# One store of early sums becomes sixteen, and moves from the end of the DMA queue to behind the fourth load

## The chip, the cores and the metric

The kernel runs on one core of a Trainium2 chip. The metric is the device time of one execution in microseconds; lower is better. The times are medians over runs, and a profile of one execution goes with them.

## The reference

`x` has the shape 32 x 512 x 1024 in float32, 67.1 MB. Each row of 1024 values is clamped at zero from below and summed:

```python
def reference(x):
    relu_x = np.maximum(x, 0)
    return np.sum(relu_x, axis=-1).astype(np.float32)
```

The output has 16384 sums, 65.5 KB. So nearly all of the traffic is the reading of `x` from HBM, and every byte of it is used once.

## The kernel before, in words

The rows are dealt out to the 128 partitions of SBUF. The first 2048 rows are the first block: partition p holds rows 16p to 16p+15. The other 14336 rows are dealt out likewise, 112 to a partition. The 128 columns of the tile `res` (128 partitions x 128 float32) hold the sums: columns 0 to 15 are those of the first block, 16 to 125 follow, and the last two columns come from the very end of the kernel.

The program is written by hand engine by engine; no scheduler moves anything. Each engine works through its own list in order, and semaphores tie the lists together.

- **Loads.** All of them are issued by SP (SyncE, line 103), in one hardware queue. Seven loads of 8.4 MB, 16 rows of 4 KB for each partition, go in turn into the three buffers `io0`, `io1` and `io2` (`NBUF` is 3). From the fourth on, a load waits until ScalarE and VectorE have read what its buffer held before; the list `freed` keeps the counts for that, and `freed[0]` is the pair of counts at which the first block's sums are complete. Here the wait is placed on VectorE's semaphore `dve`. Behind the seven follow six smaller ones: 8 rows, 4 rows, and four pieces of the last 4 rows.
- **Arithmetic of the large loads.** ScalarE clamps a buffer in place (`clamp`, line 144), in one instruction of 16 rows or in two of 8 or 7, and VectorE sums each of them over the row (`total`, line 152).
- **Arithmetic of the small loads.** Single rows are split between the engines: on ScalarE clamp and sum are one instruction (`act_row`, line 159), on VectorE too (`dve_row`, line 167). The last row is cut into pieces that ScalarE (line 121), VectorE (lines 126 and 254) and, for the clamp of one piece, GpSimd (line 234) share.
- **Stores.** SP issues three (line 115), all of them in the same hardware queue as the loads and behind the last of these: columns 0 to 15, columns 16 to 125, and the last two columns. In SP's list a wait for ScalarE's count stands ahead of each of the first two (line 114), and a wait for VectorE's count is part of the store itself.

So SP's list is: three loads; four loads, each of which waits for VectorE; the load of 8 rows, which waits as well; five small loads; store, store, store; and a last wait until the semaphore `stored` has counted 16 for every store.

A DMA of 128 partitions raises its semaphore in 16 steps, one for each DMA engine that has finished its part. The trace keeps a time for each of these steps; they are called landings here.

The call that issues the first block's sums, behind the six small loads, and the calls around it are:

```python
    store(0, ROWS, freed[0][0], sems.dve, freed[0][1])
    store(ROWS, NT - ROWS - 2, sums_act, sems.dve, sums_dve)
```

Of the kernel before, what the change touches and what calls it, by code (L numbers as in the profile page):

```python
# [7 lines left out]
P = 128  # L8

ROWS = 16  # L10
NBUF = 3
# [14 lines left out]
MIDDLE_ACT, END_ACT = 214, 321  # L26

EARLY = 1


def kernel(tc: tile.TileContext, x: bass.AP, out: bass.AP):
    nc = tc.nc
    sems = Semaphores(tc)

    tc.close()
    tc.compile()
    nc.cur_bb = nc.bb_map[tc.start_bb_name]
    body = nc.cur_bb.bb.instructions
    ends = list(body)
    body.clear()  # L40
    n_stores = relu_sum(nc, sems, x, out)
    body.extend(ends)


    nc.cur_bb = nc.bb_map[tc.start_bb_name + "_end"]
    nc.cur_bb.bb.instructions.clear()
    nums = sorted(s.num for s in (*sems.loads, sems.act, sems.dve))
    cleared = range(nums[0], nums[-1] + 1)
    assert len(cleared) == len(nums)
    nc.sync.sem_clear(cleared)  # L50
    nc.sync.wait_ge(sems.stored, 16 * n_stores).then_inc(sems.stored, -16 * n_stores)
    open_without_barrier(tc, EARLY)

# [11 lines left out]
def relu_sum(nc, sems: Semaphores, x: bass.AP, out: bass.AP):  # L65
# [23 lines left out]
    def rows(m, n):  # L89
        if m < ROWS:  # L90
            return xf[:, m : m + n, :]
        return xv[:, m - ROWS : m - ROWS + n, :]

    def sums(m, n):
        if m < ROWS:
            return of[:, m : m + n], res[:, m : m + n]
        return ov[:, m - ROWS : m - ROWS + n], res[:, m : m + n]
# [3 lines left out]
    def load(dst, src, after=None):  # L101
        nonlocal n_load
        dma = nc.sync.dma_start(out=dst, in_=src)  # L103
        if after:
            dma.wait_op(sems.dve, after[1], "sem-ge")
        dma.then_inc(sems.loads[n_load], 16)
        n_load += 1
        return sems.loads[n_load - 1]

    def store(m, n, act, sem, count):  # L110
        nonlocal n_store
        dst, src = sums(m, n)
        if act:
            nc.sync.wait_ge(sems.act, act)
        nc.sync.dma_start(out=dst, in_=src).wait_op(sem, count, "sem-ge").then_inc(
            sems.stored, 16
        )
        n_store += 1

    def act_part(ap, accum_out, after):  # L120
        nc.scalar.activation(out=ap, in_=ap, func=RELU, accum_out=accum_out).wait_op(  # L121
            *after, "sem-ge"
        ).then_inc(sems.end, 1)
# [15 lines left out]
    def clamp(ap, loaded):  # L139
        nonlocal n_act  # L140
        if n_act == 0:
            nc.scalar.preload_act_table(RELU).wait_op(loaded, 16, "sem-ge")  # L142
            loaded = None
        i = nc.scalar.activation(out=ap, in_=ap, func=RELU)  # L144
        if loaded is not None:
            i.wait_op(loaded, 16, "sem-ge")
        i.then_inc(sems.act, 1)
        n_act += 1

    def total(ap, m, n):  # L150
        nonlocal n_dve
        nc.vector.tensor_reduce(  # L152
            out=res[:, m : m + n], in_=ap, axis=mybir.AxisListType.X, op=ADD
        ).wait_op(sems.act, n_act, "sem-ge").then_inc(sems.dve, 1)
        n_dve += 1

    def act_row(ap, accum_out, loaded):
        nonlocal n_act
        i = nc.scalar.activation(out=ap, in_=ap, func=RELU, accum_out=accum_out)  # L159
        if loaded is not None:  # L160
            i.wait_op(loaded, 16, "sem-ge")
        i.then_inc(sems.act, 1)
        n_act += 1

    def dve_row(ap, accum_out, loaded):
        nonlocal n_dve
        i = nc.vector.tensor_scalar(  # L167
            out=ap,
            in0=ap,
            scalar1=0.0,  # L170
            scalar2=None,
            op0=MAX,
            op1=ADD,
            accum_out=accum_out,
        )
        if loaded is not None:
            i.wait_op(loaded, 16, "sem-ge")
        i.then_inc(sems.dve, 1)
        n_dve += 1

    freed = []
    m = 0
    for j in range(NB):
        buf = bufs[j % NBUF]
        loaded = load(buf[:, :, :], rows(m, ROWS), j >= NBUF and freed[j - NBUF])
        c = 0
        act_waits = dve_waits = loaded
        for n in TWO[j]:
            clamp(buf[:, c : c + n, :], act_waits)
            total(buf[:, c : c + n, :], m + c, n)  # L190
            act_waits = None
            c += n
        for _ in range(ACT[j]):
            act_row(buf[:, c, :], res[:, m + c : m + c + 1], act_waits)
            act_waits = None
            c += 1
        for _ in range(DVE[j]):
            dve_row(buf[:, c, :], res[:, m + c : m + c + 1], dve_waits)
            dve_waits = None
            c += 1  # L200
        assert c == ROWS
        freed.append((n_act, n_dve))
        m += ROWS
# [4 lines left out]
    for n in TAIL:  # L208
# [12 lines left out]
    src = rows(m, 4).rearrange("p c d -> p (c d)")  # L221
# [13 lines left out]
        out=clamped, in0=clamped, scalar1=0.0, scalar2=None, op0=MAX  # L235
    ).wait_op(loaded, 16, "sem-ge").then_inc(sems.end, 1)
    for lo, hi, n, first, second in (
        (end, 4 * D, END_ACT, 2 + n_last, 3 + n_last),
        (head, middle, MIDDLE_ACT, 0, 1),
    ):  # L240
        loaded = load(flat[:, at + lo : at + hi], src[:, lo:hi])
        act_part(flat[:, at + lo : at + lo + n], last[:, first : first + 1], (loaded, 16))
        dve_part(flat[:, at + lo + n : at + hi], last[:, second : second + 1], (loaded, 16))
# [2 lines left out]

    store(0, ROWS, freed[0][0], sems.dve, freed[0][1])
    store(ROWS, NT - ROWS - 2, sums_act, sems.dve, sums_dve)  # L250


# [2 lines left out]
        out=clamped,  # L255
# [5 lines left out]
        accum_out=res[:, NT - 2 : NT - 1],  # L261
    ).wait_op(*all_there, "sem-ge").then_inc(sems.end, 1)
    act_part(last[:, 2 + LAST_DVE :], res[:, NT - 1 : NT], all_there)
    store(NT - 2, 2, 0, sems.end, 16 + 5 + 2)
    return n_store


def open_without_barrier(tc: tile.TileContext, n_loads: int):

    SP = mybir.EngineType.SP
    blocks = tc.nc.main_func.blocks
    opening = blocks[0].instructions
    body = next(b for b in blocks if b.name == tc.start_bb_name).instructions
    for i in list(opening):
        if isinstance(i, (mybir.InstDrain, mybir.InstEventSemaphore)):
            opening.remove(i)
    loads = [i for i in body if i.engine == SP][:n_loads]
    for i in loads:  # L280
        assert isinstance(i, mybir.InstDMACopy)
        body.remove(i)
    at = next(n for n, i in enumerate(opening) if i.engine == SP)
    opening[at:at] = loads
# [30 lines left out]
```

## Time and profile before

| what | value |
|---|---|
| median of 3 runs | 160.91 us (160.89 to 160.95) |
| span of the profiled execution | 159.7 us |
| median of the runs less that span | 1.2 us |
| VectorE busy | 118.8 us, 74% of the span |
| ScalarE busy | 103.6 us, 65% |
| GpSimd busy | 1.0 us, 1% |
| DMA packets | 2304, 67.18 MB, mean 421 GB/s |
| read from and written to HBM | 67.11 MB and 0.07 MB |

The profile is of one execution. Its span runs from the first of the kernel's own instructions to the last; the time of a run has in it also what lies before and behind, so the median is read beside the span and not as the same thing. In the timeline, SP's rows stand for the issue of a DMA only; when its data has arrived is told by the landings. DMA issues have in the page a median time from issue to landing, and this includes the wait in the queue behind earlier DMAs: the store of the first block's sums took 31.0 us by that count, the last store, which meets empty queues, 1.4 us.

The page's row of DMA occupation in 40 slices goes over 16 engines; packet records in the trace have a start, a duration and a size each, without the number of the engine.

### The profile page before, as it was taken

What the parts mean: (1) busy time and instruction counts of PE and PEld (TensorE: products, weight loads), DVE (VectorE), ACT (ScalarE), POOL (GpSimd) and SP (SyncE); (2) the same over time, 40 slices, a digit from 0 to 9 for tenths busy, and PEclk for the clock granted to TensorE, in tenths of its full rate; (3) what the DMA queues carried; (4) which work ended last, traced back from release to release, by engine and by line L of the source; (5) the groups of instructions that cost most, each with busy time, mean ns of one, the idle gap of its engine ahead of it and who ended that gap; (6) DMA issues with size and microseconds to landing.
All of it is one profiled execution on the core that took longest, in us unless ns stands there. A gap on an engine that the chain in (4) does not pass through costs nothing.

```text
span 159.7 us, 125 instructions
## 1 busy us (share of the span) xinstructions
DVE 118.8 (74%) x44; ACT 103.6 (65%) x53; POOL 1.0 (1%) x5
## 2 busy tenths in 40 slices
DVE  0000000006999799999999999999999799999986
ACT  0000049993699808996099951999329993496995
POOL 0000000000000000000000000000000000000001
DMA  7996996996997997979969969969969969898993
GB/s 263 525 525 263 525 509 279 525 509 279 525 476 312 525 443 345 525 328 460 525 279 509 525 263 525 525 263 525 509 279 525 492 295 525 353 435 386 407 409 128
DMA packets 2304, 67.18 MB, mean 421 GB/s; under 512 B 640, under 2 KB 768, under 8 KB 1024
## 3 DMA queue, kind: packets, MB, share of 16 engines
q1 hardware_dynamic: 2304, 67.18, 98.0%
HBM read 67.11 MB, written 0.07 MB: 421 GB/s over the span
## 4 chain that ended last, share of the span: by engine, by line
DVE 45%; DMA 45%; ACT 9%; SPq 1%; issue 0%
DMA io<-in_x_dram 45%; DVE res L152 43%; ACT io L144 9%; DVE io L167 1%; SPq L103 1%; DVE io L126 1%; DVE io L254 0%
## 5 line engine op out<-in xcount | busy, mean ns | idle before, releaser
L152 DVE TENSOR_REDUCE res<-io 128x8 f32<-128x8192 f32 (+2 forms) x10 | 101.1, 10175 | 38.9 <-ACT io L144 38.9
L144 ACT ACTIVATE io<-io 128x8192 f32<-128x8192 f32 (+2 forms) x10 | 81.8, 8218 | 25.9 <-DMA io<-in_x_dram 25.9
L159 ACT ACTIVATE io<-io 128x1024 f32<-128x1024 f32 x18 | 18.8, 1043 | 6.6 <-DMA io<-in_x_dram 6.6
L167 DVE TENSOR_SCALAR_CACHE_REDUCE io<-io 128x1024 f32<-128x1024 f32 x14 | 16.2, 1214 | 0.5 <-DMA io<-in_x_dram 0.4
L142 ACT ACT_TABLE_LOAD x1 | 1.3, 1283 | 22.0 <-DMA io<-in_x_dram 22.0
L159 ACT ACTIVATION_READ_ACCUMULATOR io<-io 128x1 f32 x18 | 3.4, 187 | 0.0
L234 POOL TENSOR_SCALAR io<-io 128x254 f32<-128x254 f32 x1 | 0.8, 840 | 155.1 <-DMA io<-in_x_dram 155.1
L167 DVE DVE_READ_ACCUMULATOR io<-io 128x1 f32 x14 | 1.1, 82 | 0.0
L126 DVE TENSOR_SCALAR_CACHE_REDUCE io<-io 128x552 f32<-128x552 f32 (+1 forms) x2 | 1.1, 596 | 0.0
L121 ACT ACTIVATE io<-io 128x321 f32<-128x321 f32 (+1 forms) x2 | 0.9, 426 | 0.1
L254 DVE SCALAR_TENSOR_TENSOR io<-last,io 128x254 f32<-128x254 f32 x1 | 0.4, 425 | 0.0
L121 ACT ACTIVATION_READ_ACCUMULATOR io<-io 128x1 f32 x2 | 0.4, 187 | 0.0
L121 ACT ACTIVATE last<-last 128x153 f32<-128x153 f32 x1 | 0.3, 332 | 0.0
L121 ACT ACTIVATION_READ_ACCUMULATOR last<-last 128x1 f32 x1 | 0.2, 187 | 0.0
L126 DVE DVE_READ_ACCUMULATOR io<-io 128x1 f32 x2 | 0.2, 84 | 0.0
L299 POOL MEMSET const-bfloat16-1.0<- 128x1 bf16 x1 | 0.1, 101 | 0.0
L299 POOL MEMSET const-uint8-127<- 128x1 uint8 x1 | 0.1, 101 | 0.0
L299 POOL MEMSET const-float32-0.0<- 128x1 f32 x1 | 0.1, 99 | 0.2 <-issue 0.2
L299 POOL MEMSET const-float32-1.0<- 128x1 f32 x1 | 0.1, 98 | 0.0
L254 DVE DVE_READ_ACCUMULATOR io<-last,io 128x1 f32 x1 | 0.1, 83 | 0.0
## 6 DMA issues: line engine op xcount, KB each, us to landing
io<-in_x_dram SPq DMA_DIRECT2D x1, 4096.0 KB, 23.8
io<-in_x_dram SPq DMA_DIRECT2D x1, 2048.0 KB, 28.3
io<-in_x_dram SPq DMA_DIRECT2D x1, 1151.0 KB, 30.6
io<-in_x_dram SPq DMA_DIRECT2D x1, 436.5 KB, 31.2
io<-in_x_dram SPq DMA_DIRECT2D x1, 259.0 KB, 31.4
last<-in_x_dram SPq DMA_DIRECT2D x1, 201.5 KB, 31.4
io<-in_x_dram SPq DMA_DIRECT2D x7, 29.1
out_dram<-res SPq DMA_DIRECT2D x1, 55.0 KB, 1.6
```

The lines of the kernel that those rows point to most:

```text
L103: dma = nc.sync.dma_start(out=dst, in_=src)
L121: nc.scalar.activation(out=ap, in_=ap, func=RELU, accum_out=accum_out).wait_op(*after, "sem-ge").then_inc(sems.end, 1)
L126: i = nc.vector.tensor_scalar(out=ap, in0=ap, scalar1=0.0, scalar2=None, op0=MAX, op1=ADD, accum_out=accum_out,)
L142: nc.scalar.preload_act_table(RELU).wait_op(loaded, 16, "sem-ge")
L144: i = nc.scalar.activation(out=ap, in_=ap, func=RELU)
L152: nc.vector.tensor_reduce(out=res[:, m : m + n], in_=ap, axis=mybir.AxisListType.X, op=ADD).wait_op(sems.act, n_act, "sem-ge").then_inc(se ...
L159: i = nc.scalar.activation(out=ap, in_=ap, func=RELU, accum_out=accum_out)
L167: i = nc.vector.tensor_scalar(out=ap, in0=ap, scalar1=0.0, scalar2=None, op0=MAX, op1=ADD, accum_out=accum_out,)
L234: nc.gpsimd.tensor_scalar(out=clamped, in0=clamped, scalar1=0.0, scalar2=None, op0=MAX).wait_op(loaded, 16, "sem-ge").then_inc(sems.end, 1)
L254: nc.vector.scalar_tensor_tensor(out=clamped, in0=last[:, : 2 + LAST_DVE], scalar=0.0, in1=clamped, op0=MAX, op1=ADD, accum_out=res[:, NT ...
L299: nc = _bacc.Bacc("TRN2", target_bir_lowering=False, num_devices=1)
```

## The change

The store of the first block's sums (columns 0 to 15 of `res`, 64 bytes of each partition) no longer stands behind the last load. A new function issues it directly behind the fourth load, in 16 stores of consecutive partitions: 15 of them, then 14, 13 and so on down to 1, and then the last 8. Together these are the 128 partitions. The same bytes go to the same places. Each store has its own wait for VectorE's count and adds its 16 to `stored`; a wait for ScalarE's count stands once ahead of all of them. The lists of the other engines are unchanged, and so is the order of the loads among themselves.

```diff
+PARTS = [15, 14, 13, 12, 11, 10, 9, 8, 7, 6, 5, 4, 3, 2, 1, 8]
...
+    def store_by_parts(done):
+        nonlocal n_store
+        dst, src = sums(0, ROWS)
+        nc.sync.wait_ge(sems.act, done[0])
+        p = 0
+        for n in PARTS:
+            nc.sync.dma_start(out=dst[p : p + n], in_=src[p : p + n]).wait_op(
+                sems.dve, done[1], "sem-ge"
+            ).then_inc(sems.stored, 16)
+            n_store += 1
+            p += n
+        assert p == P
...
         loaded = load(buf[:, :, :], rows(m, ROWS), j >= NBUF and freed[j - NBUF])
+        if j == NBUF:
+            store_by_parts(freed[0])
...
-    store(0, ROWS, freed[0][0], sems.dve, freed[0][1])
     store(ROWS, NT - ROWS - 2, sums_act, sems.dve, sums_dve)
```

## The prediction

> **What bounds the kernel now.** I read the page first, then the chain of waits, the sync engine's own waits, its timeline, and last the trace's records of single DMA packets and landings. The page's queue row and two stretches of the windows view (columns: DVE, ACT, POOL busy with counts, clock, DMA share, GB/s):
>
> ```profile
> span 159.7 us, 125 instructions
> q1 hardware_dynamic: 2304, 67.18, 98.0%
> ```
>
> ```profile
> 100.00:137.00 37.00, 36.05 (x5) 27.65 (x8) 0.00 (x0) 1.00 0.98 425
> 137.00:155.00 18.00, 17.93 (x27) 15.63 (x30) 0.00 (x0) 1.00 1.00 426
> ```
>
> The 16 DMA engines are occupied for 98% of the span, and in the windows after 100 us nothing is left of them. VectorE is nearly as full there, but the page shows it at 74% over the span, and in the chain of waits the last stretch hangs on DMA again:
>
> ```profile
> 124.87 30.59 DMA io<-in_x_dram
> 155.46 0.02 issue
> 155.48 1.23 DVE io L167 x2
> 156.71 1.07 DVE io L126 x4
> 157.78 0.02 issue
> 157.80 0.43 DVE io L254 x2
> ```
>
> From 155.46 on each step starts as its load lands. The packet records say the same more sharply: every engine runs its 64 KB packets at 2.42 us each, the next one starting at the end of the one before, from 1.0 us to the last load. So the end is: the last landing of the last load (157.75), 0.5 us of arithmetic, the last store (issue 158.26, landing 159.66). A load's 16 landings, one an engine, are not level. Counted back from the latest engine, those of the last load are 0.58, 0.50, 0.48, 0.46, 0.45, 0.43, 0.42, 0.41, 0.41, 0.39, 0.39, 0.33, 0.30, 0.27, 0.21 and 0 us. One engine is always last, by 0.27 us at the first load and 0.21 at the last. It got its lag at the start (its first packet begins at 1.40 us and takes 3.30, where no other ends so late) and goes at the common pace afterwards. Delay on any other engine is free up to its figure in this list; delay on the latest one is paid in full.
>
> **The change, part by part.** *Removed from the tail: one store of 128 packets of 64 bytes.* In the tail it is issued at 126.91 and lies in every ring behind the last load. Its own landings (157.35 to 157.92) come 0.17 to 0.20 us after the last load's on the same engine, and nobody waits for them before 159.66. The final store, issued at 158.26, meets empty rings: the second store landed by 158.29, and the final one's packets begin at 159.09. So taking it away frees nothing on the path. Could it hold back the last load's landing? Between a load's last packet record and its landing lie 0.46 us on the latest engine for the last load, 0.42 to 0.50 for the six before it, 0.34 to 0.39 for the first load. I take 0; the bound for a gain is 0.46 - 0.34, 0.1 us.
>
> *Added on SP: 16 issues between the fourth and the fifth load.* The timeline of SP:
>
> ```profile
> 54.42 0.33 SPq L103 DMA_DIRECT2D io<-in_x_dram  x1
> ```
>
> ```profile
> 72.46 0.33 SPq L103 DMA_DIRECT2D io<-in_x_dram  x1
> ```
>
> ```profile
> 124.02 2.28 SPq L103 DMA_DIRECT2D io<-in_x_dram  x5
> 126.34 0.44 SPq L103 DMA_DIRECT2D last<-in_x_dram  x1
> 126.91 0.40 SPq L115 DMA_DIRECT2D out_dram<-res  x1
> ```
>
> The stores wait for the same counts of ScalarE and VectorE that have just released the fourth load, so none of the 17 waits (one for ScalarE, 16 for VectorE) waits. Issues back to back start 0.48 us apart (124.39 to 126.34, four of them). 16 x 0.48 = 7.7 us: SP is done at 54.8 + 7.7 = 62.5. What is queued behind is the fifth load, and VectorE releases its buffer only at 72.46. That is 10 us of cover. A second cover follows: engines have the fourth load to work on until 79.0 to 79.6, and a packet starts 1.0 us after its issue (first load), so the fifth load could go out 5.5 us later still. The stores may cost 23/16 = 1.45 us each on SP before an engine idles. I take 0. Later loads wait for VectorE as before, with growing reserve (the next is issued at 89.64 and reached at 98.3). The 16 x 17 more counts on the final semaphore come long before 159.66, and that wait is one instruction either way.
>
> *Added in the rings: the packets, now ahead of the fifth load.* This is where the change can reach the end, since whatever an engine does there shifts all its later packets. The only prices shown are those of the store in the tail: 64-byte packets start 7 ns apart on an engine and the closing 4-byte packet takes 6 to 7 ns more (their durations, 11 and 9 ns, overlap). Each of the 16 stores brings one closing packet to each engine that it uses. How a store of fewer than 128 partitions is spread no row shows; every DMA of before has 128 and lands on 16 engines. Bounds: one packet per engine, where the busiest engine gets 16 x (7 + 6) = 0.21 us and the idlest 0; evenly, 8 x 7 + 16 x 6 = 0.15 us on each; everything on one engine, 128 x 7 + 16 x 6 = 0.99 us. I take the first, since 128 partitions land as 8 to each of 16 engines, one landing an engine. With sizes from 15 down to 1 and then 8 the shares then run from 16 packets to none, mean 8. The latest engine could be any of them, so it pays 0 to 0.21 us, as a middle value 8 x 13 ns = 0.10 us. Even the worst other engine ends at most 0.21 - 0.21 = 0 behind it.
>
> [...] The trace shows one late engine but no number for it, and its packets are not slower after the first one.
>
> *Sum.* 0 (tail) + 0 (SP) + 0.10 (rings) on the profiled 159.7 us of span; the median of the runs, 160.91, lies 1.2 us above that span, outside of which nothing changes. 160.91 + 0.10 = 161.0. The two bounds of this case, 160.8 (a gain of 0.1) and 161.12 (0.21), both lie within 0.2% (0.32 us), about what a measurement of this kernel can tell from no change.
>
> **Rivals.**
>
> *Each store's completion holds its engine (slower).* In the tail, a store's landing follows the landing of the load ahead of it by 0.17 us or more, though the closing packets are recorded only 0.06 us apart. Read as a store that can't finish until what is ahead has, 16 stores in a row on one engine take 16 x 0.17 = 2.7 us instead of 0.21. Less the lead of that engine (0 to 0.58) this ends 2.1 to 2.7 us later: 163.0 to 163.6. It decides from 0.056 us a store (16 x 0.056 = 0.58 + 0.32) if the busiest engine is the earliest one, and from 0.32 / 16 = 0.02 us if it is the latest. For: the latency to HBM is real, and 16 closings in a row are not seen anywhere. Against: closings of loads hold nothing (a load of 8 packets takes 19.35 us a period, 8 x 2.417 = 19.34), and in the tail the second store's packets on the latest engine start at about 157.7, before the first store's landing there at 157.92. The other reading, that a write to HBM is answered 0.11 us later than one to SBUF while the engine goes on, fits as well. Chance 0.21.
>
> [...]
>
> *The fixed time of each store is served in sequence.* The last store takes 1.4 us from issue to landing; 16 of those on one engine, 22 us, would give about 183 us. [...] Against: the closings above. Chance 0.02.
>
> *A whole store goes to one engine.* 0.99 us, less a lead of 0 to 0.58: 161.3 to 161.9. For: odd sizes such as 13 and 11 have no precedent in the trace. Against: 128 rows are dealt out in equal shares. Chance 0.10.
>
> *SP is held back.* At 126.91 eight DMAs are unfinished and SP still issues in 0.4 us, so eight are accepted; the change puts up to 18 in the rings. If nine were too many, the seventh store would go out at 60.65 (a load lands), the other nine after 80.0, and 9 x 0.48 + 0.33 + 1.0 us put the fifth load's first packet at 85.7, where the engines ran dry at 79.6: about 6 us, 167. Against: in packets, eight DMAs of 9 an engine (72) are more than the change's 2 x 9 + 32 = 50. Chance 0.07.
>
> *Faster.* Only if the early engines' delay lets the latest one catch up its 0.21 us and the last landing also comes 0.1 us sooner, 160.6, does it reach the bound. The engines' equal 2.42 us speaks against shared limits. Chance 0.05.
>
> **How the numbers follow.** Forecast (0 to 0.21 us lost, or up to 0.1 gained) 0.55; the slower rivals 0.21 + 0.02 + 0.10 + 0.07 = 0.40; faster 0.05. The time is that of the likeliest, 161.0, whose own range is 160.8 to 161.15. For 8 in 10 the range takes in the one-engine case and the held engine, up to 163.6; left out are 0.02 + 0.07 above and 0.05 below.
>
> **What would show it.** Right: SP ends its 16 issues near 62.5 and the fifth load still goes out at 72.5; the engines' packets run on across 79 to 80 us with shifts up to 0.21 us; the last load's final landing lies at 157.75 to 157.96; the chain keeps its form. Wrong: landings of the fifth load spread over more than 0.8 us (they now span 0.62) would be the held engine, or all on one if one alone moves by a microsecond; a hole in the DMA row near 80 us with the fifth load issued after 72.5 would be SP; a last landing before 157.6, the gain.

## The result, and the profile after

The changed kernel takes 162.84 us (162.78 to 162.98, 4 runs) beside 160.93 us of the kernel before: a ratio of 1.0119 (95% interval 1.0107 to 1.0132), 1.9 us slower. The forecast was 161.0, no change that can be told, and the time lies outside that forecast's own range of 160.8 to 161.15. The case that came was the first of the rivals, the held engine, priced at 163.0 to 163.6; the range up to 163.6 was drawn to take it in.

From the page of the changed kernel, and the same two windows as before:

```profile
span 161.5 us, 140 instructions
q1 hardware_dynamic: 2416, 67.18, 97.4%
```

```profile
100.00:137.00 37.00, 34.25 (x5) 28.27 (x8) 0.00 (x0) 1.00 1.00 434
137.00:155.00 18.00, 17.93 (x24) 13.83 (x27) 0.00 (x0) 1.00 0.95 406
```

The bytes are the same, and the 112 further packets are closings, the 4-byte packets that end a DMA on an engine (16 stores have 128, the one store had 16). By their records the DMA engines are about as full as before, 97.4% and 98.0%, but a held packet counts as busy in this, as is shown below. What has changed is seen where ScalarE waits. The timeline between 98 and 103 us, of the kernel before and then of the changed one:

```profile
99.38 7.03 ACT L144 ACTIVATE io<-io 128x8192 f32<-128x8192 f32 x1 [5.40 <-DMA io<-in_x_dram]
```

```profile
101.17 7.03 ACT L158 ACTIVATE io<-io 128x8192 f32<-128x8192 f32 x1 [7.28 <-DMA io<-in_x_dram]
```

The fifth load, the one behind the stores, lands 1.79 us later (its last landing is at 101.15, before at 99.36), and nothing later gives that back or adds to it: the last load lands at 159.51 instead of 157.75, the last store at 161.45 instead of 159.66. The chain of waits of the changed kernel, in parts:

```profile
72.37 28.78 DMA io<-in_x_dram
101.15 0.02 issue
101.17 7.04 ACT io L158
...
126.41 30.86 DMA io<-in_x_dram
157.26 0.02 issue
157.29 1.23 DVE io L181 x2
```

The fifth load is now a link of the chain by itself. In the kernel before, VectorE's sums filled this place of the chain, up to 124 us:

```profile
55.21 68.79 DVE res L152 x7
```

SP is not the reason:

```profile
54.30 0.33 SPq L104 DMA_DIRECT2D io<-in_x_dram  x1
54.76 5.70 SPq L127 DMA_DIRECT2D out_dram<-res  x16
```

```profile
72.37 0.37 SPq L104 DMA_DIRECT2D io<-in_x_dram  x1
```

The 16 issues end at 60.5 and the fifth load goes out at 72.37, when VectorE lets go of its buffer, as before. The loss begins on the engines, right behind the stores, which they reach at about 79 us. Two windows, of the kernel before and then of the changed one (the last two columns are DMA share and GB/s, and a large packet counts in the window in which it starts):

```profile
80.00:82.00 2.00, 2.00 (x2) 1.97 (x1) 0.00 (x0) 1.00 1.13 492
```

```profile
80.00:82.00 2.00, 2.00 (x2) 2.00 (x1) 0.00 (x0) 1.00 0.53 229
```

Fewer than half as many bytes are begun there as before.

The packet records show the place. On each engine the stores' packets pass at the expected pace, 13 ns for a packet and a closing, and the first 64 KB packet of the fifth load starts right behind. But that packet doesn't take 2.42 us everywhere. The records don't name the engine. But an engine's first packet of the fifth load starts 13 ns for each store behind the end of its last packet of the fourth, and matching ends and starts over all 16 engines gives each its number of stores (no engine has 8):

| stores on the engine | 16 | 15 | 14 | 13 | 12 | 11 | 10 | 9 | 7 | 6 | 5 | 0 to 4 |
|---|---|---|---|---|---|---|---|---|---|---|---|---|
| us over 2.42 | 2.04 | 1.75 | 1.68 | 1.45 | 1.50 | 1.40 | 1.21 | 1.12 | 0.43 | 0.25 | 0.08 | 0 |

The first four cost nothing. From 5 to 16 stores each costs (2.04 - 0.08) / 11 = 0.18 us on average, but not evenly: 0.17 to 0.18 up to 7, 0.69 for the two between 7 and 9, and (2.04 - 1.12) / 7 = 0.13 from 9 on. All packets after this one take 2.42 us again, to within 0.05. The engine with 16 stores has been made the last one: its own lead over the latest engine was 0.31 us, and 2.04 + 0.21 - 0.31 = 1.94 us is what the load loses by this. The landings show 1.79; in the profile of the changed kernel the fourth load had landed 0.09 us earlier (79.92, before 80.01).

### The profile page after: what moved, and what is told of

Its sections match the earlier page's. It is cut to its first block, busy times and chain, and to the rows that moved or that the text cites. A ratio compares the mean times of both kernels' runs of the same rounds, so it can differ in the third digit from the quotient of the medians.

```text
span 161.5 us, 140 instructions
## 1 busy us (share of the span) xinstructions
DVE 118.8 (74%) x44; ACT 103.5 (64%) x53; POOL 1.0 (1%) x5
## 3 DMA queue, kind: packets, MB, share of 16 engines
q1 hardware_dynamic: 2416, 67.18, 97.4%
## 4 chain that ended last, share of the span: by engine, by line
DMA 62%; DVE 23%; ACT 13%; SPq 1%; issue 0%
DMA io<-in_x_dram 62%; DVE res L166 21%; ACT io L158 13%; DVE io L181 1%; SPq L104 1%; DVE io L140 1%; DVE io L269 0%
```

## The experiments

The theory when the runs were planned: each DMA that ends on an engine holds it by about 0.13 us (the slope from 9 to 16 stores), however few bytes it has; four or five in a row are covered, and the engine with the most of them sets the time. Rivals: the place (any store ahead of a load costs), the 64-byte packets, HBM's answer to a write, the number of stores, a limit that the engines share. All ratios are against the kernel before on the same chip.

**e1_one_store: the move without the split.**

```diff
-PARTS = [15, 14, 13, 12, 11, 10, 9, 8, 7, 6, 5, 4, 3, 2, 1, 8]
+PARTS = [128]
```

> The store moves but is not split: one store of 128 partitions behind the fourth load, 8 packets and one closing on each of the 16 engines. Held engine (each store's completion holds the engine that it is on, about 0.13 us each, the first four or five without effect): one completion on each engine, so no loss beyond the 0.06 us of the packets; 160.9 to 161.0. Rival, the place is what costs (a store ahead of a load delays that load whatever its form): about the whole 1.9 us, 162.8. A third, that each 64-byte packet to HBM holds the engine 0.13 us: 8 of them on every engine, 0.5 to 1.0 us, 161.4 to 161.9.

161.04 us, ratio 1.0007 (0.9998 to 1.0016): no difference. Every first packet of the fifth load takes 2.42 us. The place costs nothing, and eight 64-byte packets an engine don't either.

**e3_four_places: the same stores, four behind each of four loads.**

```diff
-        if j == NBUF:
-            store_by_parts(freed[0])
+        if j >= NBUF:
+            store_by_parts(freed[0], j - NBUF)  # PARTS[4 * k : 4 * k + 4]
```

> The same 16 stores, but four behind each of the fourth to the seventh load (15, 14, 13, 12; then 11 to 8; 7 to 4; 3, 2, 1, 8), so that no engine has more than four in a row. Held engine with the first four free at each place: 160.9 to 161.1. Held engine without a free part (0.13 us for every store wherever it stands): the busiest engine still has 16, 162.5 to 162.9. If the time depends on the number of stores alone: 162.8.

161.09 us, ratio 1.0009 (0.9999 to 1.0018). The first packets behind the stores take at most 0.14 us more. So 16 stores of these shapes, and 16 closings on one engine, are free when no more than four follow one another. The number of stores is not the cause; the row of them is.

**e5_tiny_loads: loads of the same shapes instead of stores.**

```diff
-        dst, src = sums(0, ROWS)
+        dst, src = spare[:, :], rows(0, 1)[:, 0, :ROWS]
...
+    store(0, ROWS, freed[0][0], sems.dve, freed[0][1])
     store(ROWS, NT - ROWS - 2, sums_act, sems.dve, sums_dve)
```

> In the place of the 16 stores stand 16 loads of the same shapes (15 x 64 bytes and so on) from the input to a tile that nobody reads, and the one store of the sums is back behind the last load. If any DMA's completion holds its engine: 162.5 to 162.9, as with stores. If only the answer of HBM to a write does: 160.9 to 161.2, the 0.21 us of packets at most. A delay in between, 161.3 to 162.3, would say that the hold is the way of the data, HBM to SBUF here, with another length.

162.63 us, ratio 1.0109 (1.0092 to 1.0126). The longest first packet takes 1.98 us more than 2.42, with the stores it was 2.04. The direction hardly matters here, and the answer of HBM to a write is not the cause.

**e8_one_engine: as many closings on one engine, a quarter of them in all.**

```diff
-PARTS = [15, 14, 13, 12, 11, 10, 9, 8, 7, 6, 5, 4, 3, 2, 1, 8]
+PARTS = [1] * 16 + [112]
```

> Sixteen stores of 1 partition each and one of 112, in the same place: 32 closings over all engines instead of 128, but still 17 on one engine. Held engine, each for itself: one engine is late by 17 stores, about 2.0 us in its first packet of the fifth load, the others by nothing; 162.7 to 163.1. If the loss is a limit that all engines share (so many small writes to HBM or semaphores in a time), a quarter of the closings costs a quarter: 161.2 to 161.5.

162.84 us, ratio 1.0119 (1.0104 to 1.0134), the changed kernel's own. One first packet takes 2.01 us more, the other 15 nothing; the fifth load's landings are 98.87 to 99.46 on 15 engines and 101.25 on the last. So each engine is held for itself, and one held engine is enough. With the other engines quiet, the landings of the stores on this one can be read off singly: 80.47, 80.66, 80.84, 81.02, 81.20, 81.39, 81.58, 81.77, 81.96, 82.15, 82.33, 82.52, 82.70. One every 0.18 to 0.19 us, though their packets were recorded 13 ns apart. That is also the average price of a store in the table, 0.18 us.

**e2_parts_at_end: the 16 stores in the place of the one, behind the last load.**

```diff
-        if j == NBUF:
-            store_by_parts(freed[0])
...
-    store(0, ROWS, freed[0][0], sems.dve, freed[0][1])
+    store_by_parts(freed[0])
     store(ROWS, NT - ROWS - 2, sums_act, sems.dve, sums_dve)
```

> The 16 stores stand where the one store stood, behind the last load. Held engine: with the changed kernel the last of the 16 landed 2.6 us behind its load; here that is about 160.2, and the second and the last store, whose packets were at 157.6 to 159.3, stand behind it on the busiest engine: the end comes 0.6 to 0.9 us later, 161.5 to 161.9. If only a large load behind the stores suffers: 160.9 to 161.0.

162.07 us, ratio 1.0068 (1.0053 to 1.0083), 1.1 us where 0.6 to 0.9 were expected. No load stands behind the stores here, and the time is lost all the same: the last store is issued at 158.34 (before at 158.26), but the last landing is at 160.58 and not 159.66. That the hold needs a large load behind it is excluded. The timeline of SP has something else:

```profile
126.48 0.44 SPq L104 DMA_DIRECT2D last<-in_x_dram  x1
127.05 21.95 SPq L127 DMA_DIRECT2D out_dram<-res  x16
156.83 1.86 SPq L116 DMA_DIRECT2D out_dram<-res  x2
```

The 16 issues take 22 us instead of 5.7. The first five go out at 0.34 to 0.43 us each, the sixth takes 0.8, the seventh 4.8. At that point, by a count from the lists of DMAs, the busiest engine has some 5 packets of the seventh load, 6 x 9 of the smaller loads and 5 x 2 of the stores ahead of it, 69 in all. SP's wait costs nothing here, since its next work comes at 156.8.

**e4_127_and_1: two stores.**

```diff
-PARTS = [15, 14, 13, 12, 11, 10, 9, 8, 7, 6, 5, 4, 3, 2, 1, 8]
+PARTS = [127, 1]
```

> Two stores in the same place, of 127 and of 1 partition. If 127 partitions go to one engine, that engine has 127 packets and two closings. Held by the DMA, not by the packet: 128 x 7 ns = 0.9 us of packets, of which some 0.6 is covered as the first four stores were: 160.9 to 161.6. Held by each 64-byte packet: 128 x 0.13 = 17 us, 177. If they are spread over 16 engines after all, nothing: 160.9, and the first packets of the fifth load would all take 2.42 us.

163.03 us, ratio 1.0129 (1.0112 to 1.0146), and for a reason that no expectation had. Timeline of SP, and windows of DMA work:

```profile
54.74 24.76 SPq L127 DMA_DIRECT2D out_dram<-res  x2
79.55 27.50 SPq L104 DMA_DIRECT2D io<-in_x_dram  x3
```

```profile
79.00:79.50 0.50, 0.50 (x1) 0.00 (x0) 0.00 (x0) 1.00 0.06 4
79.50:80.00 0.50, 0.50 (x1) 0.09 (x1) 0.00 (x0) 1.00 0.10 9
80.00:80.50 0.50, 0.50 (x1) 0.50 (x1) 0.00 (x0) 1.00 0.04 4
80.50:81.00 0.50, 0.50 (x2) 0.50 (x1) 0.00 (x0) 1.00 5.36 1835
```

The second store's issue lasts 24.4 us, from 55.11 to 79.50, and the fifth load goes out at 79.55 instead of 72.4. Its first packet starts at 80.53, while 15 engines ran dry at 79.0 to 79.4: in the windows up to 80.50 the DMA share (the column before the last) is 0.10 and less. A large packet counts in the window in which it starts, so the last window has more than 1. This is the rival that held SP back, in another kernel. What was to be learned can still be read: the store of 127 partitions has a single landing of an engine, its packets pass one after the other 7 ns apart, and the engine that had them stands out in nothing: the fifth load's landings spread over 0.5 us (100.81 to 101.31). A hold for each packet, 17 us, is excluded. A single short hold would not be seen here, since the engines stood idle before the fifth load.

**e6_eight_of_16 and e7_four_of_32: the same number of closings on every engine.**

```diff
-PARTS = [15, 14, 13, 12, 11, 10, 9, 8, 7, 6, 5, 4, 3, 2, 1, 8]
+PARTS = [16] * 8    # e6; e7: [32] * 4
```

> Eight stores of 16 partitions, so one packet and one closing of each store on each engine: 8 on all 16 engines, 128 closings in all as in the changed kernel. Held engine, each for itself: the first packet of the fifth load is 0.6 to 1.0 us longer on every engine (0.43 at 7 stores and 1.12 at 9 in the changed kernel); 161.5 to 161.9. If all engines share the limit: 128 closings cost what they cost in the changed kernel, 162.8.

> Four stores of 32 partitions in the same place: two packets and one closing of each on all 16 engines, four closings an engine. Held engine with the first four free, as the changed kernel's engines with four stores and the kernel with four places showed: no first packet of the fifth load over 2.42 us by more than 0.1, 160.9 to 161.1. If the eight stores of 16 cost in proportion to their number (0.77 us there): 161.3.

Eight: 161.75 us, ratio 1.0050 (1.0035 to 1.0065); the first packets take 0.46 to 0.96 us more on all 16 engines, between the 0.43 of 7 and the 1.12 of 9 stores in the changed kernel. It has the changed kernel's 128 closings and 40% of its loss. Four: 161.07 us, ratio 1.0006 (0.9996 to 1.0015), at most 0.11 us more. With one store (e1) these make a curve: 1 and 4 closings an engine are free, 8 cost 0.8 us, 16 cost 1.9.

**e9_4kb_loads and e10_4kb_rows: is the time added to the data's own?**

```diff
-        dst, src = spare[:, :], rows(0, 1)[:, 0, :ROWS]
+        dst, src = spare[:, :], rows(0, 1)[:, 0, :]   # e9: 4 KB, rows 64 KB apart
+        dst, src = spare[:, :], x_flat[:P, :]         # e10: consecutive rows
```

> As with the 16 tiny loads, but 4 KB for each partition instead of 64 bytes, so that each packet needs 0.15 us by the pace of the large loads (64 KB in 2.42 us); 0.5 MB of reading comes on top, 16 packets or 2.5 us of it on the busiest engine. A DMA occupies its engine for a least time within which its own data passes: only these 2.5 us are seen, 163.0 to 163.5. A fixed time beside the data: 2.5 + 2.0 us, 165.0 to 165.5.

> The 16 loads of 4 KB for each partition again, but from consecutive rows: before, their rows lay 64 KB apart, all 16 engines took 0.3 us for a packet of 4 KB and even the engines with few of these loads lost 2.5 us, so that time told of the rows' places too. Least time within which a DMA's own data passes: 16 packets of 0.15 us are 2.4 us of data on the busiest engine and all that is seen, 163.0 to 163.5. A fixed 0.13 us beside the data: 2.4 + 2.0, 165.0 to 165.5. If the rows' places were not the cause: 165.7 again.

165.75 us, ratio 1.0297 (1.0282 to 1.0312), and 166.0 us, ratio 1.0312 (1.0283 to 1.0341). Neither tells: even the engines that came first to the fifth load, those with few of these loads, had first packets 1.8 to 2.6 us longer, which neither theory has. The rows' places in HBM were not the reason for that, as e10 shows. I then supposed the narrow range of partitions that the loads write to.

**e12_rows_64b and e11_rows_4kb: the same question with every engine treated alike.** The diff is against e10.

```diff
-        dst, src = spare[:, :], x_flat[:P, :]
+        for k in range(16):
+            dst, src = spare[k % 8 :: 8, k // 8, :], x_flat[16 * k : 16 * k + 16, :16]   # e11: :1024
```

> In the place of the 16 stores: 16 loads of 16 partitions, 64 bytes each, into a tile that nobody reads; the partitions are 8 apart, so that every engine gets one packet and one closing of each load and the writes lie over all of SBUF. The one store is back at the end. Held engine: all 16 engines have 16 closings in a row, and the first packet of the fifth load is 1.6 to 2.1 us longer on each; 162.5 to 163.0. If the 16 loads on all engines get in each other's way (256 closings instead of 128): above 163.5.

> The same loads with 4 KB for each partition: 16 packets of 0.15 us more on every engine, 2.4 us of data, without the narrow range of partitions that the two earlier kernels with 4 KB wrote to. A least time for a DMA on its engine, within which its own data passes: the loss is the data alone, 2.3 to 2.7 us, 163.3 to 163.7. A fixed time beside the data: 2.4 us and the loss of the kernel with 64 bytes, 4.2 to 4.6 us, 165.1 to 165.6. If all engines again lose 5.0 us with packets of 0.3 us: the partitions' range was not the cause of that.

With 64 bytes 163.43 us, ratio 1.0146 (1.0129 to 1.0162), 2.3 us; the first packets take 1.73 to 2.53 us more on all 16 engines. That is 0.4 us above the expectation; the closings are twice as many here, so a small shared part is possible, and wasn't separated. With 4 KB 165.62 us, ratio 1.0284 (1.0268 to 1.0299): 4.5 us, close to the data (2.4) and the loss with 64 bytes (2.3) together. The packets show where it goes: the first one or two on each engine take 159 ns, the later ones about 275 (median), 0.12 us more. So the hold looks like a time beside the data's own: the data alone would have given 163.3 to 163.7. This is not shown beyond doubt, since the 4 KB packets of e9 and e10 were slow as well (a median of 310 ns in e9), for a reason that wasn't found.

## Why the prediction was right and wrong

The time of 162.84 us lies in the stated range, and the forecast of 161.0 was wrong in its mechanism. The range holds it because its upper end was set by the held engine, a rival with a chance of 0.21; of the sum itself, the rings' term failed. The sign that the prediction named for the held engine came: landings of the fifth load spread over more than 0.8 us. They spread over 2.27 (98.88 to 101.15).

*Right.* The tail: the removed store freed nothing (e1, with the store moved whole, took 161.04 us). SP: 16 issues, 5.7 us instead of the 7.7 estimated, behind VectorE's release and at no cost. The spread over the engines, 16 packets on the busiest and none on another, was a guess from the 8 packets an engine that 128 partitions have, and it fits the records of all 16 engines. For 127 partitions it doesn't hold: in e4 they went to one engine (a single landing, packets 7 ns apart). Which number the engines have, no run here shows.

*Wrong: the term "added in the rings".* It was sized at 0.10 us with 0.21 as its bound; the kernel lost 1.9, and the engine with the most stores 2.04 beside the 0.21. The price came from the tail store's records, 7 ns a packet and 6 to 7 a closing. Those records are kept to the nanosecond in the changed kernel, 13 ns a store, and the engine is held all the same; the hold appears in the *duration of the next large packet*. A packet's record was not the whole time for which it took its engine up: in e8 the stores' packets are recorded 13 ns apart and land 0.18 to 0.19 us apart.

*Wrong: the two arguments against the held engine.* That loads' closings hold nothing was true (19.35 us a period for eight packets of 2.417), and didn't bear: one closing between two large loads lengthened no first packet in e1, four in a row lengthened one by at most 0.11 us in e7 and 0.14 in e3. That the second store's packets begin before the first one has landed (157.7 and 157.92 in the kernel before) was true as well, and fits records that run ahead of what holds the engine.

*The row that had it.* The 0.17 us by which the tail store landed behind its load was the price; e8 measured 0.18 to 0.19. I gave that reading 0.21 because another one, an estimate from the same 0.17, fitted the row equally (HBM answers a write 0.11 us later than SBUF); no run shows such a delay. e5 separates the two: loads into SBUF cost as much (1.98 us on the longest first packet, 2.04 with the stores). As for the rival's size, 2.1 to 2.7 us against 1.9: its price of 0.17 was about right, and what failed is that all 16 stores pay it. With the first four free it gives 12 x 0.17 = 2.04 us, the longest packet's own figure; that the two agree to the last digit is chance, since the table is not a straight line. A small slip bears on nothing: the final semaphore counts 15 x 16 more, not 16 x 17, since one store becomes 16.

*The other rivals.* "A whole store goes to one engine": not with these shapes. "SP is held back": not in the changed kernel, whose 18 unfinished DMAs were accepted (no store's issue took over 0.42 us); where SP did wait, in e2 and e4, my count of the packets on one engine fits better (below). Its count of 50 packets for the change had been the right argument. "The fixed time in sequence", 22 us: no.

*Open.* Whether the closing holds the engine or the end and begin of a DMA as such: every DMA here has a closing, and all the small DMAs raise the same semaphore, `stored`. The landings 0.18 us apart on one engine (e8) go with either, and no run took the closing away. Why four are covered is not shown: a closing's record runs 0.42 to 0.50 us ahead of its landing (the latest engine at the six loads before the last, in the kernel before), which at 0.18 us each would cover two or three. Nor is the jump between 7 and 9 stores explained; e5 has it too, with no first packet between 0.39 and 1.04 us over 2.42. And e9 and e10, where all engines were slowed, remain unexplained.

## What to carry to other kernels

Count the DMAs, not the bytes or the packets, that one engine has to finish in a row: up to four small ones between large transfers were free here (at most 0.14 us on a first packet in e3, 0.11 in e7, neither to be told in the time), and from the fifth to the sixteenth each delayed that engine, and with it the whole next load, by 0.18 us on average. The store cut into parts of 15 partitions down to 1 put 16 endings on one engine and none on another, and the fifth load's last landing, at 101.15, was that of the worst of them, where the first was at 98.88. Where small DMAs must be many, place a few behind each large load, as e3 did (161.09 us, where the changed kernel took 162.84); and read a price for a DMA from the landings and from the next packet's duration (0.18 us here), not from its own records (13 ns for a packet and a closing).

## What the runs showed of the hardware

- Small DMAs in a row on one engine land 0.18 to 0.19 us apart (e8); small loads in the place of the stores cost as much (e5: 1.98 us on the engine with 16, against 2.04).
- SP's issue waited when one engine had about 70 packets ahead of it. That figure is my estimate, a count from the lists of DMAs; no view shows how many packets an engine has waiting. Some 69 were accepted in 0.4 us in the kernel before, the store that met 69 in e2 took 0.8 us and the one behind it 4.8, and a store that put 127 on one engine (e4) held SP's next issue for 24.4 us, so that the other 15 engines, dry at 79.0 to 79.4, had nothing until 80.53. The number of DMAs doesn't explain it: the changed kernel's 18 were accepted, the last of them in 0.28 us.
- An issue on SP took 0.42 us for a store of 16 partitions (e6) and 0.25 us for one of 1 (e8), and in the changed kernel 0.42 for 15 and 0.25 for 1. It was no longer above 16: 0.42 to 0.43 for 32 (e7), and 0.32 for the 127 that went to one engine (e4).
- The lag of the latest engine is no property of the kernel: between the last two landings of the fourth load lie 0.24 us in the kernel before, 0.19 in the changed one and 0.02 in e1, though nothing in their programs differs up to there. Whether it goes with the chip or with the execution, the runs don't show.
